# A two-layer conformer and attention trunk: a second half's products and sums of squares on VectorE, two early products ahead of the down projections

## The chip, the cores and the metric

The kernel runs on one core of a Trainium2 chip. Its time is device microseconds of one execution; given is the median of several executions. A core has five engines with an instruction stream each: TensorE (PE), VectorE (DVE), ScalarE (ACT), GpSimd (POOL) and SyncE (SP). Each issues its instructions in order and waits on semaphores for the others. Transfers are issued by SyncE (hardware queues) and by GpSimd (the software queue) and run beside the engines.

## The reference

A trunk of two layers over 512 tokens of width 1024, all in float32. Layer 0 is a conformer convolution and a SwiGLU feed-forward network (FFN); layer 1 is windowed attention over shared keys and values and a second FFN. The change touches the FFN of layer 0.

```python
def swiglu_ffn(x, w_up, w_down):
    gate, up = jnp.split(x @ w_up, 2, axis=-1)
    return (jax.nn.silu(gate) * up) @ w_down
...
def reference(...):
    h = x                                  # (1, 512, 1024) float32
    for l in range(2):
        if l < 1:
            h = h + conformer_conv(rmsnorm(h, norm_mix[l]), ...)   # pw1 + GLU, causal depthwise 31, LayerNorm, silu, pw2
        else:
            kv = rmsnorm(h, norm_kv) @ w_kv
            ...
            q = (rmsnorm(h, norm_mix[l]) @ w_q[j]).reshape(B, S, N_HEADS, HEAD_DIM)
            attn = banded_sink_attention(q, k_shared, v_shared, sinks[j], rel_bias)
            h = h + attn @ w_o[j]
        h = h + swiglu_ffn(rmsnorm(h, norm_ffn[l]), ffn_w_up[l], ffn_w_down[l])   # 1024 -> 2 x 2816 -> 1024
    return rmsnorm(h, norm_final)
```

## The kernel before

All activations stay on the chip, transposed (channels on the partitions, tokens along the free axis). Weights, about 250 MB of reads with their sums, are streamed in chunks of 128 x 1024 float32 (512 KB). A chunk goes through a fixed chain: SyncE loads it into one of six `raw` buffers (line 260; `load` runs nine chunks ahead of use), ScalarE casts it to the matmul's number format (`whi`, line 293), VectorE subtracts that from the original (`wlo`, line 296), at most three chunks ahead of use and with four buffers each, and TensorE multiplies. A product in full precision is three matmuls (`mm3`, lines 381 to 383): high weights by high activations, high weights by low activations, low weights by high activations. One chunk is 24 matmuls of 128x256. `PLAN` fixes the order of the chunks.

The FFN of layer 0 runs in this order. **Part 0**: the output projection of the convolution (`pw2`) and the ups, the gated product and the downs of hidden pairs 0 to 2, for the first 256 tokens. Then **twelve early products** (`FIRST`): pairs 3 to 10 are computed by a Strassen-like scheme of seven block products instead of eight (`SEVEN`); some of its products need the first half's tokens alone, and they are computed here and copied aside (line 1245). **Part 1**: `pw2` and pairs 0 to 2 for the second 256 tokens, in a "twin" form (`mm2`, two terms side by side). Then the remaining products of pairs 3 to 10 for all tokens, and their downs.

Behind TensorE run background jobs: a job is a generator, with points (chunk number, steps done) by which `pace` advances it. The convolution of the second half of tokens is such a job (`second`) during part 0 and the early products; `Rows0.sums`, which forms sums of activation blocks (`plain`, `rows`, lines 1283, 543, 546), is one during part 1.

The lines around the change:

- `evac` (lines 627 to 641) turns the banks of one pair into hidden activations. In the twin form: ScalarE copies half of a bank (632), VectorE adds the other (633), GpSimd multiplies by the inverse root mean square (635), ScalarE applies silu (636), GpSimd multiplies gate and up (637), ScalarE casts the high half (640), VectorE subtracts for the low half (641). Three pairs make six GpSimd products of 128x512.
- `Rms.add` (line 492) sums the squares of eight tiles for the norm, on the engine `eng` that it was given: GpSimd for the second half of tokens. Line 508 is the power that gives the inverse root mean square, on GpSimd.
- Four of the seven products use sums of weight blocks (`S1` to `S4`). They are formed in DRAM by transfers: a copy issued by SyncE (`copy_sums`, line 274) and a transfer that adds onto it, issued by GpSimd (`prepare`, line 288: `sum<-in_W` and `sum<-sum`). The latter is placed behind the last GpSimd operation that was marked by `pool_op`:

```python
            with tc.issue_after(pooled[0]):
                nc.gpsimd.dma_start(summed[c], chunk(c, SUMS[c[2]][1]), accum_op=ALU.add, max_dma_last_dim=4096)
```

Within these constraints a scheduler with a simulated timeline decides the order of the instructions of each engine.

Of the kernel before, what the change touches and what calls it, by code (L numbers as in the profile page):

```python
# [18 lines left out]
P = 128  # L19
# [18 lines left out]
FIRST = [(4, "A11"), (3, "A12"), (4, "A12"), (5, "A11"), (8, "A12"), (5, "A12"),  # L38
         (6, "A11"), (9, "A12"), (6, "A12"), (7, "A11"), (10, "A12"), (7, "A12")]
LAST = FT // 2 - 1  # L40
# [22 lines left out]
def ups(pair):  # L63
    return [("up", 0, pair, half, which) for half in range(2) for which in range(2)]
# [25 lines left out]
def chunk_plan():  # L90
# [7 lines left out]
    def downs(lo, hi):  # L98
        for g in range(2):
            for kp in range(lo, hi):  # L100
                plan.append(("down", 0, kp, g))

    for part in range(2):
        pw2()
        for pair in range(*HALVES0[0]):
            plan.extend(ups(pair))
        downs(*HALVES0[0])
        if part == 0:
            plan.extend(("up0", *step) for step in FIRST)
    for group in GROUPS0:  # L110
# [98 lines left out]
def hybrid_trunk(ctx: ExitStack, tc: tile.TileContext, xT, W, prm_in, wdw_in, sinks, relb, onehot, fin, lead, out):  # L209
# [54 lines left out]
    def pool_op(op):  # L264
        pooled[0] = op.ins
        return op
# [325 lines left out]

    def ffn_part(layer, part, xg, tok, rms, on_h=None, twin=False, plain=None):
        lo, hi = HALVES0[part]
        hid = ffn_up(layer, lo, hi, xg, tok, rms, twin, plain)
        w = tok.stop - tok.start
        for g in range(2):
# [22 lines left out]
    def ffn_up(layer, lo, hi, xg, tok, rms, twin=False, plain=None):  # L620
# [3 lines left out]
        def evac(pair, banks):  # L624
            rs_bc = rms.step2()
            if twin:
# [7 lines left out]
                t1v, t2v = (t.rearrange("p (a s) -> p a s", a=2) for t in (t1, t2))  # L634
                nc.gpsimd.tensor_mul(t1v, t1v, rs_bc.unsqueeze(1).to_broadcast([P, 2, w]))
                nc.scalar.activation(t1, t1, AF.Silu)
                pool_op(nc.gpsimd.tensor_mul(t2, t1, t2))
                i = 2 * (pair - lo)
# [268 lines left out]
    with tc.tile_pool(name="conv", bufs=2) as cv:  # L907
# [307 lines left out]
        with tc.issue_after(h0.silu):  # L1215
            late.gate()
        h1.after = [h0.silu]
        base = seen[0]
        job(second, (base, 0), (base + 8, 17), (base + 13, 20), (base + 26, 34), (base + 36, 40), (base + 39, 43), (base + 40, 44),
            (base + 41, 44), (base + 42, 45), (base + 43, 46), (base + 45, 48), (base + 46, 49), (base + 50, h1.n_steps - early))  # L1220
        x0 = {"ffn0": Pairs(KT)}
# [4 lines left out]
        preparing[0], share[0] = prepare(), 0.5  # L1226
        ffn_part(0, 0, x0["ffn0"], HALF[0], n0.rms, plain=plain)
        for _ in range(2):
            let_go()
        room = [q[:, n, :] for q in (quad(F32), quad(F32)) for n in range(4)]  # L1230
        room[4:4] = [keep.tile([P, 512], F32, tag="c11", name=uid("c11")) for _ in range(4)]
        room = [t.rearrange("p (a s) -> p a s", a=2) for t in room]
        first = {pair: {"A12": room[n]} for n, pair in enumerate(range(*HALVES0[1]))}
        for n, pair in enumerate(FIRST11):
            first[pair]["A11"] = room[8 + n]
        chains = {}
        for n, (pair, a) in enumerate(FIRST):
            pace()
            if n < 2:
                let_go()  # L1240
            begins = pair not in chains
            r = chains.setdefault(pair, new_chain() if begins else None)
            j = 4 * (a == "A12")
            product(("up0", pair, a), [[x0["ffn0"][j + k][e][:, HALF[0]] for k in range(4)] for e in range(2)], r, begins, pace)
            nc.scalar.copy(first[pair][a], r)  # L1245
        flush()
# [52 lines left out]
    plain1 = z0.tile([P, KT, W2], F32, tag="z0", name=uid("plain1"), bufs=4)  # L1299
    n1 = Next(("ffn0",), x0, bc0, HALF[1])  # L1300
    base = seen[0]
# [401 lines left out]
```

## Time and profile before

| | us |
|---|---|
| median of three runs | 1044.0 (1043.18, 1044.06, 1044.0) |
| profiled execution, its time | 1043.35 |
| profiled execution, its span | 1041.6 |
| TensorE busy | 1029.7 (99%) |
| VectorE busy | 794.5 (76%) |
| ScalarE busy | 603.4 (58%) |
| GpSimd busy | 455.3 (44%) |
| mean granted TensorE clock | 0.998 |

The span is what the profiler saw of that one execution; 1.75 us of its time lie outside it. A row of the timeline is start, duration, engine, line, operation, output<-input, and in brackets how long the engine had been idle and who released it. A busy TensorE counts matmuls whose ends are modelled and overlap, so what it lost is read from start to start. Part 0's downs begin at about 203 us, the early products follow them; the twin's ups end at about 303, and part 1's downs run on to about 330.

### The profile page before, as it was taken

To read this page: it belongs to the slowest core of one execution; us is meant where nothing else is said; L and a number is where in the kernel's file an instruction comes from. 1 tells how busy PE (TensorE), PEld (TensorE's weight loads), DVE (VectorE), ACT (ScalarE), POOL (GpSimd) and SP (SyncE) were. 2 spreads that over 40 slices of the span, in tenths; PEclk is the share of its full clock that TensorE was granted. 3 is DMA by queue.
4 is the path that set the end of the run, shared out by engine and by line. 5 is a ranking of instruction groups with operands and counts; after the bars stand their busy time and mean duration, and the time that the engine had idled before them with its cause. 6 is when DMAs were issued, how large, how long until landed. Compare 5 with 4: busy or idle time off the path is not lost.

```text
span 1041.6 us, 17905 instructions
## 1 busy us (share of the span) xinstructions
PE 1029.7 (99%) x6676; PEld 935.2 (90%) x6676; DVE 794.5 (76%) x1228; ACT 603.4 (58%) x1044; POOL 455.3 (44%) x557
## 2 busy tenths in 40 slices
PE   9999999999999999999999999999999999999996
PEld 8888889999989998899888877789989999898995
DVE  3999988986889795487567556678786877869686
ACT  3887796857574552256353555468645546554653
POOL 3999997752343233033234255501470333223134
PEclk9999999999999999999999999999999999999999
DMA  9999847999999999889998987977699897655642
GB/s 358 329 325 260 151 130 228 274 255 245 268 234 286 324 317 289 239 250 342 316 323 263 236 226 206 234 224 221 203 300 298 250 253 211 199 184 185 193 150 81
DMA packets 68243, 256.73 MB, mean 246 GB/s; under 512 B 7835, under 2 KB 14140, under 8 KB 67132
## 3 DMA queue, kind: packets, MB, share of 16 engines
q1 hardware_dynamic: 54044, 204.95, 57.0%
q0 software_dynamic: 13824, 50.34, 26.3%
q8 instruction: 52, 0.85, 0.3%
q10 hardware_dynamic: 288, 0.31, 0.1%
q14 instruction: 35, 0.29, 0.1%
HBM read 250.32 MB, written 105.91 MB: 342 GB/s over the span
## 4 chain that ended last, share of the span: by engine, by line
PE 94%; DVE 3%; DMA 2%; issue 1%; ACT 0%; POOLq 0%; POOL 0%; ACTq 0%; DVEq 0%
PE bank L381 20%; PE bank L382 20%; PE bank L383 20%; PE bank L933 10%; PE bank L878 9%; PE bank L379 4%; PE bank L413 2%; DMA raw<-sum 1%; PE bank L1437 1%; PE bank L1479 1%; PE bank L1466 1%; DVE wlo L296 1%; PE bank L414 1%; PE bank L1031 1%; PE bank L1612 1%
## 5 line engine op out<-in xcount | busy, mean ns | idle before, releaser
L293 ACT CAST whi<-raw 128x1024 fp32r<-128x1024 f32 x246 | 256.5, 1048 | 275.1 <-PE bank L382 181.0
L296 DVE TENSOR_TENSOR wlo<-raw,whi 128x1024 fp32r<-128x1024 f32 x246 | 317.6, 1299 | 117.3 <-ACT whi L293 116.5
L381 PE MATMUL bank<-quad,whi 128*128 128x256 f32 (+1 forms) x1016 | 315.8, 314 | 0.3 <-ACT quad L1245 0.2
L382 PE MATMUL bank<-quad,whi 128*128 128x256 f32 (+1 forms) x1016 | 315.5, 312 | 0.4 <-DVE quad L546 0.4
L383 PE MATMUL bank<-quad,wlo 128*128 128x256 f32 (+1 forms) x1016 | 314.5, 312 | 0.9 <-DVE wlo L296 0.9
L829 POOL TENSOR_TENSOR up<-up 128x512 f32<-128x512 f32 x38 | 71.8, 1889 | 345.9 <-ACT up L826 319.3
L381 PEld LDWEIGHTS bank<-quad,whi 128*128 128x128 f32 x1016 | 192.9, 191 | 13.1 <-issue 1.3
L383 PEld LDWEIGHTS bank<-quad,wlo 128*128 128x128 f32 x1016 | 193.0, 191 | 12.4 <-DVE wlo L296 1.1
L382 PEld LDWEIGHTS bank<-quad,whi 128*128 128x128 f32 x1016 | 193.4, 191 | 11.6 <-DVE quad L546 0.6
L975 POOL TENSOR_TENSOR pr<-pr,pr 128x256 f32<-128x256 f32 x208 | 155.4, 794 | 6.6 <-ACT pr L974 6.5
L381 PE MATMUL bank<-rows,whi 128*128 128x256 f32 x544 | 154.0, 284 | 0.7 <-ACT whi L293 0.4
L382 PE MATMUL bank<-rows,whi 128*128 128x256 f32 x544 | 153.6, 283 | 0.0
L383 PE MATMUL bank<-rows,wlo 128*128 128x256 f32 x544 | 153.4, 283 | 0.0
L982 DVE SCALAR_TENSOR_TENSOR bank<-apad,wdw,bank 128x256 f32<-128x256 f32 x248 | 112.4, 485 | 3.3
L974 ACT ACTIVATE pr<-apad,wdw 128x256 f32<-128x256 f32 x208 | 98.2, 501 | 14.6 <-POOL pr L975 12.7
L381 PEld LDWEIGHTS bank<-rows,whi 128*128 128x128 f32 x544 | 103.5, 191 | 1.9 <-ACT whi L293 0.6
L382 PEld LDWEIGHTS bank<-rows,whi 128*128 128x128 f32 x544 | 103.7, 191 | 0.5 <-issue 0.2
L383 PEld LDWEIGHTS bank<-rows,wlo 128*128 128x128 f32 x544 | 103.6, 191 | 0.0
L933 PE MATMUL bank<-quad,w 128*128 128x256 f32 x448 | 98.7, 380 | 0.0
L933 PEld LDWEIGHTS bank<-quad,w 128*128 128x128 f32 x448 | 84.9, 190 | 11.8 <-DVE bank L982 0.2
L878 PE MATMUL bank<-wlo,fhi 128*128 128x512 f32 x140 | 55.3, 395 | 0.0
L492 POOL TENSOR_TENSOR tmp<-tmp,tmp 128x256 f32<-128x256 f32 (+1 forms) x28 | 27.1, 969 | 64.3 <-ACT tmp L488 58.6
(231 smaller groups left out, 1550.3 us busy)
## 6 DMA issues: line engine op xcount, KB each, us to landing
raw<-in_W_dram SPq DMA_DIRECT2D x162, 512.0 KB, 5.8
raw<-sum SPq DMA_DIRECT2D x96, 512.0 KB, 4.7
sum<-in_W_dram SPq DMA_DIRECT2D x64, 512.0 KB, 7.6
sum<-in_W_dram POOLq DMA_DIRECT2D x48, 512.0 KB, 8.9
sum<-sum POOLq DMA_DIRECT2D x48, 512.0 KB, 10.3
sum<-in_W_dram SPq DMA_DIRECT2D x4, 4096.0 KB, 34.6
w<-in_W_dram SPq DMA_DIRECT2D x14, 512.0 KB, 8.9
fd<-fs SPq DMA_DIRECT2D x1, 3072.0 KB, 44.7
```

Source lines behind the costliest of these rows:

```text
L293: on_act = nc.scalar.copy(hi, src).ins
L296: latest[:] = [on_act, lo_engine[0].tensor_sub(lo, src, f32(hi)).ins]
L379: stamp[0] = nc.tensor.matmul(out, w[0], x, start=start, stop=stop).ins
L381: nc.tensor.matmul(out, w[0], x[0], start=start, stop=False, **kw)
L382: nc.tensor.matmul(out, w[0], x[1], start=False, stop=False, **kw)
L383: stamp[0] = nc.tensor.matmul(out, w[1], x[0], start=False, stop=stop, **kw).ins
L829: pool_op(nc.gpsimd.tensor_mul(gate, gate, c[:, m, :, 1, :]))
L878: nc.tensor.matmul(out, x, w[:, ws], start=first and e == 0 and i == 0, stop=e == 1 and i == 2, skip_group_check=True)
L933: mm = nc.tensor.matmul(self.pb[:, w * W2:(w + 1) * W2], w1_of(ct, w, k), x[k] if x else xg[k][:, tok], start=k == 0, stop=k == KT - 1)
L974: on_act = nc.scalar.mul(pr, a[:, j:j + W2], tap(j))
L975: on_pool = pool_op(nc.gpsimd.tensor_add(pr, acc, pr))
L982: on_dve = nc.vector.scalar_tensor_tensor(yt if i == nd - 1 else c, src, tap(i), c if i else self.shift, op0=ALU.mult, op1=ALU.add)
```

## The change

Four edits. The twin's two GpSimd products in `evac` become VectorE products, and the second of them is no longer marked by `pool_op`. The sums of squares of the second half (`n1`) are added by VectorE, and with that they too are not marked. Two of the early products run between the ups and the downs of part 0 (`mid`), the other ten behind the downs, one of them, (7, A11), two places earlier. The points of the second half's convolution between 20 and 36 steps are given in more detail. Line numbers behind the edits shift by 3 to 13.

```diff
--- before.py
+++ after.py
@@ -36,7 +36,8 @@
 GROUPS0 = ((3, 7), (7, 11))
 FIRST11 = (4, 5, 6, 7)
 FIRST = [(4, "A11"), (3, "A12"), (4, "A12"), (5, "A11"), (8, "A12"), (5, "A12"),
-         (6, "A11"), (9, "A12"), (6, "A12"), (7, "A11"), (10, "A12"), (7, "A12")]
+         (6, "A11"), (7, "A11"), (9, "A12"), (6, "A12"), (10, "A12"), (7, "A12")]
+N_MID = 2
 LAST = FT // 2 - 1
 STEPS1 = [("two", 0), ("up", 2), ("low", 0)]
 TWO = [(p, a) for a in ("A11", "A12", "S4") for p in range(2)] + [(p, a) for p in range(2) for a in ("S1", "S2", "S3", "A22")]
@@ -104,9 +105,11 @@
         pw2()
         for pair in range(*HALVES0[0]):
             plan.extend(ups(pair))
+        if part == 0:
+            plan.extend(("up0", *step) for step in FIRST[:N_MID])
         downs(*HALVES0[0])
         if part == 0:
-            plan.extend(("up0", *step) for step in FIRST)
+            plan.extend(("up0", *step) for step in FIRST[N_MID:])
     for group in GROUPS0:
         plan.extend(("up0", *step) for step in part2_products(group))
         downs(*group)
@@ -590,9 +593,11 @@
         nc.vector.tensor_mul(b, b, rs_bc)
         nc.vector.tensor_add(into, b, into)
 
-    def ffn_part(layer, part, xg, tok, rms, on_h=None, twin=False, plain=None):
+    def ffn_part(layer, part, xg, tok, rms, on_h=None, twin=False, plain=None, mid=None):
         lo, hi = HALVES0[part]
         hid = ffn_up(layer, lo, hi, xg, tok, rms, twin, plain)
+        if mid is not None:
+            mid()
         w = tok.stop - tok.start
         for g in range(2):
             if w == 256:
@@ -632,9 +637,9 @@
                         nc.scalar.copy(tm, b[:, 1, :])
                         nc.vector.tensor_add(tm, b[:, 0, :], tm)
                 t1v, t2v = (t.rearrange("p (a s) -> p a s", a=2) for t in (t1, t2))
-                nc.gpsimd.tensor_mul(t1v, t1v, rs_bc.unsqueeze(1).to_broadcast([P, 2, w]))
+                nc.vector.tensor_mul(t1v, t1v, rs_bc.unsqueeze(1).to_broadcast([P, 2, w]))
                 nc.scalar.activation(t1, t1, AF.Silu)
-                pool_op(nc.gpsimd.tensor_mul(t2, t1, t2))
+                nc.vector.tensor_mul(t2, t1, t2)
                 i = 2 * (pair - lo)
                 q = hid.q[i // 4][:, i % 4:i % 4 + 2]
                 nc.scalar.copy(q[:, :, 0, :], t2v)
@@ -1216,33 +1221,41 @@
             late.gate()
         h1.after = [h0.silu]
         base = seen[0]
-        job(second, (base, 0), (base + 8, 17), (base + 13, 20), (base + 26, 34), (base + 36, 40), (base + 39, 43), (base + 40, 44),
-            (base + 41, 44), (base + 42, 45), (base + 43, 46), (base + 45, 48), (base + 46, 49), (base + 50, h1.n_steps - early))
+        job(second, (base, 0), (base + 8, 17), (base + 13, 20), (base + 20, 27), (base + 24, 30), (base + 30, 36), (base + 36, 40),
+            (base + 39, 43), (base + 40, 44), (base + 41, 44), (base + 42, 45), (base + 43, 46), (base + 45, 48), (base + 46, 49),
+            (base + 50, h1.n_steps - early))
         x0 = {"ffn0": Pairs(KT)}
         plain = quads.tile([P, KT, W2], F32, tag="quad", name=uid("plain"))
         bc0 = new_bc()
         n0 = Next(("ffn0",), x0, bc0, HALF[0], nc.vector, plain)
         pw2(h0.z, n0)
         preparing[0], share[0] = prepare(), 0.5
-        ffn_part(0, 0, x0["ffn0"], HALF[0], n0.rms, plain=plain)
+        first, chains = {}, {}
+
+        def early_products(steps):
+            for pair, a in steps:
+                pace()
+                if held:
+                    let_go()
+                begins = pair not in chains
+                r = chains.setdefault(pair, new_chain() if begins else None)
+                k0 = 4 * (a == "A12")
+                product(("up0", pair, a), [[x0["ffn0"][k0 + k][e][:, HALF[0]] for k in range(4)] for e in range(2)], r, begins, pace)
+                nc.scalar.copy(first[pair][a], r)
+
+        def mid():
+            room = [q[:, n, :] for q in (quad(F32), quad(F32)) for n in range(4)]
+            room[4:4] = [keep.tile([P, 512], F32, tag="c11", name=uid("c11")) for _ in range(4)]
+            room = [t.rearrange("p (a s) -> p a s", a=2) for t in room]
+            first.update((pair, {"A12": room[n]}) for n, pair in enumerate(range(*HALVES0[1])))
+            for n, pair in enumerate(FIRST11):
+                first[pair]["A11"] = room[8 + n]
+            early_products(FIRST[:N_MID])
+
+        ffn_part(0, 0, x0["ffn0"], HALF[0], n0.rms, plain=plain, mid=mid)
         for _ in range(2):
             let_go()
-        room = [q[:, n, :] for q in (quad(F32), quad(F32)) for n in range(4)]
-        room[4:4] = [keep.tile([P, 512], F32, tag="c11", name=uid("c11")) for _ in range(4)]
-        room = [t.rearrange("p (a s) -> p a s", a=2) for t in room]
-        first = {pair: {"A12": room[n]} for n, pair in enumerate(range(*HALVES0[1]))}
-        for n, pair in enumerate(FIRST11):
-            first[pair]["A11"] = room[8 + n]
-        chains = {}
-        for n, (pair, a) in enumerate(FIRST):
-            pace()
-            if n < 2:
-                let_go()
-            begins = pair not in chains
-            r = chains.setdefault(pair, new_chain() if begins else None)
-            j = 4 * (a == "A12")
-            product(("up0", pair, a), [[x0["ffn0"][j + k][e][:, HALF[0]] for k in range(4)] for e in range(2)], r, begins, pace)
-            nc.scalar.copy(first[pair][a], r)
+        early_products(FIRST[N_MID:])
         flush()
 
     bias = {}
@@ -1297,7 +1310,7 @@
     part2 = ExitStack()
     z0 = part2.enter_context(tc.tile_pool(name="part2", bufs=4))
     plain1 = z0.tile([P, KT, W2], F32, tag="z0", name=uid("plain1"), bufs=4)
-    n1 = Next(("ffn0",), x0, bc0, HALF[1])
+    n1 = Next(("ffn0",), x0, bc0, HALF[1], nc.vector)
     base = seen[0]
     rows0 = Rows0(x0["ffn0"], plain, plain1)
     rows0.rms = rows0
```

The order of the instructions shows what this moves. A number behind a name counts tiles: whi_3586 and wlo_3587 are the high and the low part of one chunk. The chunks around the end of part 1 are called by running numbers: 46 to 48 (the last of them whi_3521) and 49 to 51 (whi_3553, whi_3586, whi_3625) are part 1's downs, for the first and for the second half of the output channels; 52 (whi_3656) and 53 (whi_3687) are the first chunks of the products that follow.

GpSimd, from the power of the second half's norm (rs_3214) through the twin. Before:

```order
L288 DMA sum_512<-sum_508 128x1024
L508 TENSOR_TENSOR rs_3214<-ms_3212,mhalf 128x2
L288 DMA sum_506<-in_W_dram 128x1024
L635 TENSOR_TENSOR tmp_3271<-tmp_3271,rsbc_1401 128x512
L637 TENSOR_TENSOR tmp_3272<-tmp_3271,tmp_3272 128x512
L288 DMA sum_510<-in_W_dram 128x1024
L288 DMA sum_508<-sum_506 128x1024
L635 TENSOR_TENSOR tmp_3389<-tmp_3389,rsbc_1401 128x512
L637 TENSOR_TENSOR tmp_3390<-tmp_3389,tmp_3390 128x512
L288 DMA sum_512<-sum_508 128x1024
L288 DMA sum_506<-in_W_dram 128x1024
L635 TENSOR_TENSOR tmp_3502<-tmp_3502,rsbc_1401 128x512
```

Now:

```order
L291 DMA sum_512<-sum_508 128x1024
L511 TENSOR_TENSOR rs_3214<-ms_3212,mhalf 128x2
L291 DMA sum_506<-in_W_dram 128x1024
L291 DMA sum_510<-in_W_dram 128x1024
L291 DMA sum_508<-sum_506 128x1024
L291 DMA sum_512<-sum_508 128x1024
L291 DMA sum_506<-in_W_dram 128x1024
L291 DMA sum_510<-in_W_dram 128x1024
L291 DMA sum_779<-in_W_dram 128x1024
L291 DMA sum_510<-in_W_dram 128x1024
L291 DMA sum_508<-sum_506 128x1024
L291 DMA sum_512<-sum_508 128x1024
```

The products between the transfers are gone; from rs_3214 to the first gate of the next stage eleven accumulating transfers follow one another, and nine, with no computation between them, stand ahead of it.

VectorE, in part 1's downs (wlo_3554 is chunk 49's low half, quad_3159 the last pair's hidden activations). Before:

```order
L296 TENSOR_TENSOR wlo_3522<-raw_3339,whi_3521 128x1024
L1283 TENSOR_TENSOR plain_2862<-plain_2862 128x1024
L633 TENSOR_TENSOR tmp_3503<-bank_3406,tmp_3503 128x256
L633 TENSOR_TENSOR tmp_3503<-bank_3407,tmp_3503 128x256
L296 TENSOR_TENSOR wlo_3554<-raw_3364,whi_3553 128x1024
L546 TENSOR_TENSOR rows_3557<-plain_2862,rows_3557 128x1024
L296 TENSOR_TENSOR wlo_3587<-raw_3408,whi_3586 128x1024
L641 TENSOR_TENSOR quad_3159<-tmp_3503,quad_3159 128x2x256
```

Now:

```order
L299 TENSOR_TENSOR wlo_3522<-raw_3339,whi_3521 128x1024
L1296 TENSOR_TENSOR plain_2862<-plain_2862 128x1024
L638 TENSOR_TENSOR tmp_3503<-bank_3406,tmp_3503 128x256
L638 TENSOR_TENSOR tmp_3503<-bank_3407,tmp_3503 128x256
L640 TENSOR_TENSOR tmp_3502<-tmp_3502,rsbc_1401 128x512
L299 TENSOR_TENSOR wlo_3554<-raw_3364,whi_3553 128x1024
L299 TENSOR_TENSOR wlo_3587<-raw_3408,whi_3586 128x1024
L549 TENSOR_TENSOR rows_3557<-plain_2862,rows_3557 128x1024
L642 TENSOR_TENSOR tmp_3503<-tmp_3502,tmp_3503 128x512
L299 TENSOR_TENSOR wlo_3626<-raw_3431,whi_3625 128x1024
```

The products of line 640 and 642 stand among the subtractions, and the two subtractions of chunks 49 and 50 follow one another.

TensorE, in part 1's downs, from the end of chunk 50 (whi_3586) on. Before:

```order
L383 MATMUL bank_3619<-quad_3158,wlo_3587 128x256
L381 MATMUL bank_3619<-quad_3158,whi_3586 128x256
L382 MATMUL bank_3619<-quad_3158,whi_3586 128x256
L383 MATMUL bank_3619<-quad_3158,wlo_3587 128x256
L381 MATMUL bank_3618<-quad_3159,whi_3625 128x256
L382 MATMUL bank_3618<-quad_3159,whi_3625 128x256
```

Now:

```order
L385 MATMUL bank_3619<-quad_3158,whi_3586 128x256
L386 MATMUL bank_3619<-quad_3158,wlo_3587 128x256
L384 MATMUL bank_3724<-quad_1396,whi_3656 128x256
L385 MATMUL bank_3724<-quad_1396,whi_3656 128x256
L384 MATMUL bank_3517<-quad_3159,whi_3521 128x256
L384 MATMUL bank_3518<-quad_3159,whi_3521 128x256
L384 MATMUL bank_3618<-quad_3159,whi_3625 128x256
L384 MATMUL bank_3619<-quad_3159,whi_3625 128x256
L384 MATMUL bank_3756<-rows_3370,whi_3687 128x256
L385 MATMUL bank_3756<-rows_3370,whi_3687 128x256
L386 MATMUL bank_3724<-quad_1396,wlo_3657 128x256
```

Before, chunk 51 (whi_3625) and chunk 52 followed in full, and chunk 53 (whi_3687) behind both; now two matmuls each of 52, 48 (whi_3521), 51 and 53 come first.

## The prediction

> **What bounds the kernel now.** I read the page first: its busy times, and the shares of the chain of waits.
>
> ```profile
> PE 1029.7 (99%) x6676; PEld 935.2 (90%) x6676; DVE 794.5 (76%) x1228; ACT 603.4 (58%) x1044; POOL 455.3 (44%) x557
> PE 94%; DVE 3%; DMA 2%; issue 1%; ACT 0%; POOLq 0%; POOL 0%; ACTq 0%; DVEq 0%
> ```
>
> TensorE bounds it. The change adds and removes no matmul, so it can only move the time in which TensorE stands still. The second view is the list of TensorE's waits, the third the windows by stage, of the one stage that is undisturbed and of the ones the change touches.
>
> ```profile
> PE bank L383 <- DVE wlo L296: 0.9, 1, 0.9
> PE bank L382 <- DVE quad L546: 0.4, 1, 0.4
> PE bank L381 <- ACT whi L293: 0.4, 1, 0.4
> PE bank L381 <- ACT quad L1245: 0.2, 1, 0.2
> 200.00:205.00 5.00, 4.63 (x38) 4.30 (x37) 5.00 (x8) 4.90 (x10) 4.44 (x6) 1.00 0.95 223
> 215.00:220.00 5.00, 5.00 (x44) 5.00 (x43) 5.00 (x7) 2.68 (x5) 4.52 (x5) 1.00 1.02 344
> 315.00:320.00 5.00, 4.07 (x34) 3.81 (x32) 5.00 (x5) 3.04 (x4) 3.11 (x3) 1.00 1.02 334
> 335.00:340.00 5.00, 4.51 (x35) 3.93 (x33) 2.50 (x4) 1.54 (x2) 0.00 (x0) 1.00 1.06 271
> ```
>
> The columns are length, then busy time and count for TensorE, weight loads, VectorE, ScalarE and GpSimd, granted clock, DMA share, GB/s. A full window holds 44 matmuls at clock 1.00, one each 0.114 to 0.12 us; a weight chunk of 24 matmuls therefore takes 2.88 us. In 315:320 VectorE is busy all 5.00 us and TensorE misses ten matmuls. The timeline of TensorE has the holes one by one:
>
> ```profile
> 202.78 0.28 PE L382 MATMUL bank<-quad,whi 128*128 128x256 f32 x1
> 203.43 0.38 PE L382 MATMUL bank<-quad,whi 128*128 128x256 f32 x1 [0.37 <-DVE quad L546]
> 230.78 0.28 PE L383 MATMUL bank<-quad,wlo 128*128 128x256 f32 x1
> 231.23 0.39 PE L381 MATMUL bank<-quad,whi 128*128 128x256 f32 x1 [0.17 <-ACT quad L1245]
> 317.25 0.28 PE L382 MATMUL bank<-quad,whi 128*128 128x256 f32 x1
> 318.46 0.39 PE L383 MATMUL bank<-quad,wlo 128*128 128x256 f32 x1 [0.93 <-DVE wlo L296]
> 338.73 0.28 PE L383 MATMUL bank<-rows,wlo 128*128 128x256 f32 x1
> 339.43 0.39 PE L381 MATMUL bank<-rows,whi 128*128 128x256 f32 x1 [0.42 <-ACT whi L293]
> ```
>
> Start to start minus the usual 0.12, they lose 0.53, 0.33, 1.09 and 0.58 us. The matmul behind a hole starts its successor 0.22 us later instead of 0.12, which adds 0.1 each: 0.6, 0.4, 1.2 and 0.7. A few smaller gaps lie beside the last three in these windows; from the missing matmuls I count 0.1, 0, 0.3 and 0.5 for them. So what the change can win here is 0.7 + 0.4 + 1.5 + 1.2 = 3.8 us of 1041.6, about 0.4%.
>
> **First part: two early products ahead of the downs.** The hole at 203 waits for the low half of the last pair's hidden activations. Between that pair's ups and the downs now run two products, 2 x 2.88 = 5.8 us of matmuls on data that was complete before. They cover a hole of 0.6. The same two are missing later, between the downs and the second part, where nothing was waited for that they hid: the rest of the list keeps ten. The hole at 231 is the copy of an early product standing late in ScalarE's order; with the new list that copy is issued ahead of the squares. I count both as gone, -0.7 and -0.4. If the cover fails they stay (0), and that is one bound; a product that itself waits for its weights would be the other, at most the 0.58 of the weight wait seen at 339 for each, +1.2. Weights are the reason against: at 200 to 230 loads land in 5.8 us, with nine chunks (25.9 us) issued ahead. The earlier job points of the second half's convolution move ScalarE and VectorE work by a few chunks inside 220 to 265; the full window there (x44 in 215:220) says that TensorE does not notice, so 0, with the 0.4 of the hole at 231 as its bound.
>
> ```profile
> raw<-in_W_dram SPq DMA_DIRECT2D x11, 512.0 KB, 5.8
> ```
>
> **Second part: six products and seven adds go from GpSimd to VectorE.** The price of one comes from the same shapes on VectorE, the relief from VectorE rows that overlap a GpSimd product:
>
> ```profile
> L641 DVE TENSOR_TENSOR quad<-tmp,quad 128x512 fp32r<-128x512 f32 x3 | 2.0, 679 | 0.0
> 294.38 1.47 DVE L296 TENSOR_TENSOR wlo<-raw,whi 128x1024 fp32r<-128x1024 f32 x1 [0.80 <-ACT whi L293]
> 298.16 1.66 DVE L1283 TENSOR_TENSOR t<-plain,plain 128x1024 f32<-128x1024 f32 x1
> 299.75 3.05 DVE L296 TENSOR_TENSOR wlo<-raw,whi 128x1024 fp32r<-128x1024 f32 x1
> 305.34 2.14 POOL L637 TENSOR_TENSOR tmp<-tmp,tmp 128x512 f32<-128x512 f32 x1 [3.64 <-DVE tmp L633]
> 306.25 2.31 DVE L1283 TENSOR_TENSOR plain<-plain,t 128x1024 f32<-128x1024 f32 x1
> 313.32 2.21 POOL L635 TENSOR_TENSOR tmp<-tmp,rsbc 128x512 f32<-128x512 f32 x1 [4.22 <-DVE tmp L633]
> 314.29 2.32 DVE L1283 TENSOR_TENSOR plain<-plain 128x1024 f32<-128x1024 f32 x1
> 317.42 2.13 POOL L637 TENSOR_TENSOR tmp<-tmp,tmp 128x512 f32<-128x512 f32 x1 [1.89 <-DVE tmp L633]
> 318.32 2.31 DVE L546 TENSOR_TENSOR rows<-plain,rows 128x1024 fp32r<-128x1024 f32 x1
> 323.43 1.21 DVE L1283 TENSOR_TENSOR plain<-plain 128x1024 f32<-128x1024 f32 x1
> ```
>
> A 128x512 operation is 0.68 us, 0.60 from start to start in a run of them: six cost VectorE 3.6 us. In exchange, a 1.21 us operation lasted 2.31 whenever it met a GpSimd product, and ended about 1.1 us behind it. Three of them give back 3.3 us; the lengthened operations at 294.38, 298.16 and 299.75 give 0.26, 0.45 and 1.84 more, against 1.21. Net: 3.6 - 5.8 = -2.2 us on VectorE in 290 to 325. Bounds: +3.6 without any relief, -2.2 with all of it. I take the whole relief, since each lengthened row lies beside a product; most of it falls early, where the subtractions are chunks ahead. The products also get shorter in their own chain (0.68 for some 2.1 of GpSimd), though each now stands in VectorE's order behind a weight's subtraction of 1.21, so the hidden pair is not later.
>
> The low weights that TensorE waits for at 317.25 are subtracted in VectorE's next-but-one place. There the operation at 314.29 shrinks by 1.1 and one product, 0.6, slips in ahead of that subtraction: in sum it ends some 0.8 us earlier than the 318.4 of before, still 0.2 to 0.3 late. TensorE also arrives earlier by what it won before, 1.1, which VectorE follows only in part. So of the 1.5 lost around 318 I take back 1.5 and put a remainder of 0.3 against it: bounds 0 and 1.5.
>
> The seven adds of squares (128x256) cost half of a product's 0.68 each, 2.4 us in all, around 268 to 283; the GpSimd adds there lengthened VectorE's neighbours:
>
> ```profile
> L538 DVE SCALAR_TENSOR_TENSOR quad<-h,prm,quad 128x256 fp32r<-128x256 f32 x8 | 6.8, 899 | 0.0
> L982 DVE SCALAR_TENSOR_TENSOR bank<-apad,wdw,bank 128x256 f32<-128x256 f32 x19 | 9.1, 479 | 0.1
> ```
>
> Against 479 ns the eight of L538 hold 8 x 0.42 = 3.4 us, of which I count 2 as contention. Nothing of TensorE waits here, so 0; without the relief +2.4 of VectorE time in front of chunks that are several ahead, still 0 for TensorE unless the lead is gone (below).
>
> **The accumulating transfers.** GpSimd issues the sums of weight blocks (`sum<-in_W`, `sum<-sum`) in its own order. Six of them stood behind the last product at 317.42 and left in one burst:
>
> ```profile
> 319.50 0.82 POOL L288 DMA_DIRECT2D sum<-in_W_dram  x1
> 322.15 2.38 POOL L288 DMA_DIRECT2D sum<-sum  x1
> 338.32 1.05 ACT L293 CAST whi<-raw 128x1024 fp32r<-128x1024 f32 x1 [4.35 <-DMA raw<-sum]
> 342.13 1.05 ACT L293 CAST whi<-raw 128x1024 fp32r<-128x1024 f32 x1 [2.26 <-DMA raw<-in_W_dram]
> 345.94 1.05 ACT L293 CAST whi<-raw 128x1024 fp32r<-128x1024 f32 x1 [2.27 <-DMA raw<-sum]
> raw<-sum SPq DMA_DIRECT2D x7, 512.0 KB, 15.2
> ```
>
> While they run, a weight chunk arrives every 3.81 us (338.32, 342.13, 345.94) for 2.88 of use, and its load takes 15.2 us (the last row, transfers issued in 320 to 345). In the changed order GpSimd computes nothing between 240 and 345 except one 128x2 power: nine transfers stand ahead of it, eleven behind, held only by what they read. They start earlier and are through some 15 us sooner, around 333, so that the weights for 338 land in time: -1.2. Bounds: 0, and the starvation of rival C.
>
> **A new wait.** TensorE's order at the end of part 1 changes: behind chunk 50 (whi 3586) come only six matmuls of other chunks and then chunk 53 (whi 3687), which stood 72 matmuls later. There are four buffers of high weights, and the cast of 53 needs the one of 50. Its load is the first of the four here:
>
> ```profile
> 311.46 10.66 SPq L260 DMA_DIRECT2D raw<-sum  x4
> DMA to landing us min/median/max: 6.8/10.3/17.3
> ```
>
> (the second row is all loads of raw weights issued in 308 to 332). TensorE reaches the place 45 matmuls after 317.25, at 322.65, less 1.1 won before, plus 0.3: 321.85. Landing is 311.46 + 10.3 = 321.8. The cast, 1.05 with 0.1 on each side, ends at 323.1, while six matmuls last until 322.6: 0.5 is the lower bound. At 17.3 us to land it would be 7.3. With more accumulating transfers in flight at that point than before, I take 1.1, near the median.
>
> **The sum.** -0.7 - 0.4 - 1.5 - 1.2 + 0.3 + 1.1 = -2.4 us. The profiled execution took 1043.35 us (span 1041.6), 0.65 under the median 1044.0 of three (1043.18 to 1044.06). So 1040.95 for such an execution and **1041.6 us** for the median.
>
> **The rivals.** A is the forecast. **B: the gain is eaten at chunk 53.** If its load takes 12.5 us rather than 10.3 to 11, TensorE waits 2.7 there and not 1.1: net -0.8, 1043.2. For it: the same view's maximum of 17.3 and the DMA share near 1.0 throughout; against it: the four loads of that row left one after the other as buffers came free, so an earlier VectorE also issues them earlier.
>
> **C: twenty accumulates in one stream starve the weights, slower.** At 3.81 us per chunk from 287 to 329, 11.0 chunks arrive and 14.6 are used: 3.6 chunks or 10.3 us of matmuls must come out of the lead. The lead is 25.9 us of issue-ahead less 15.2 to land, 10.7, if all nine may be in flight; six raw buffers alone, 17.3, leave 2.1. With a lead of 4, a wait of 6.3 arises: 6.3 - 2.4 = +3.9, 1047.9. It decides against the change from a lead under 7.9, and measurably under 5.8. For it: 15.2 against 5.8 us to land. Against it: a transfer that adds to a sum waits for the one before it, so the eleven cannot all run at once, and in 315:320 with four of them queued the only wait was VectorE's. The Trainium skill's page "DMA: Bandwidth & Descriptors", section "Queues, rings and completion order", says that each DMA engine serves the queues it has work for in turn, a packet at a time. By that the software queue takes its share from the weights as long as it has anything to do, whoever is urgent; the trace agrees so far, in the landing times just named.
>
> **D: VectorE becomes the bound, slower.** If the lengthened operations stay long for another reason, VectorE does 3.6 us more before the low weights at 318: the 1.5 there becomes 5.1 instead of 0.3, net -2.4 + 4.8 = +2.4, 1046.4. For it: 5.00 of 5.00 busy in 315:320. Against it: 1.21 us at 323.43 once no product ran.
>
> That the change does not do what it says is no case: the orders show both moves.
>
> **How the numbers follow.** Two readings closer than 0.2%, 2.1 us, cannot be told apart for this kernel, so faster is under 1041.9 and slower over 1046.1. A 0.60 (0.52 faster, 0.08 same, as 1041.6 stands close to the line), B 0.19 (0.16 same, 0.03 faster if the wait is only a little larger), C 0.13 and D 0.08 (0.20 slower between them, 0.01 same). Faster 0.55, same 0.25, slower 0.20. The low end is no new wait beyond 0.5 and a remainder of 0: 1041.6 - 0.6 - 0.3, and 1.0 more of the smaller gaps in these windows, 1039.7. The high end takes in B and D's 1046.4: 1046.5, with C beyond it. The forecast's own range is 1039.7 to 1042.8.
>
> **What would show it.** Right: no TensorE wait for the hidden low half near the first downs, none for an early product's copy, 128x1024 operations of VectorE at 1.21 all through the twin, accumulating transfers gone from 319 to 323, no ScalarE wait of over 2 us for a weight at 338, and a short TensorE wait for a cast of high weights at about 322. Wrong: a wait of more than 2 us for `raw<-sum` between 315 and 335 (B or C), TensorE waiting for `wlo` with VectorE at 5.00 of 5 (D), or holes in the same places as before.

## The result and the profile after

The change made the kernel slower: 1048.16 us median of six runs (1047.41 to 1048.84) against 1043.63 for the kernel before on the same chip (1043.18 to 1044.06), a ratio of 1.0043 (95% interval 1.003 to 1.0056), +4.5 us. The forecast was 1041.6 with a range up to 1046.5. The profiled execution, the slowest of the six, took 1048.84 us; its span is 1047.0.

The page's busy times and chain, then the list of TensorE's waits (who waits, for whom; sum, times, longest):

```profile
PE 1032.8 (99%) x6676; PEld 938.1 (90%) x6676; DVE 793.7 (76%) x1241; ACT 603.9 (58%) x1044; POOL 436.9 (42%) x544
PE 96%; DMA 2%; DVE 1%; issue 0%; ACT 0%; POOLq 0%; SPq 0%; POOL 0%; DVEq 0%; ACTq 0%
```

```profile
PE bank L384 <- ACT whi L296: 2.5, 1, 2.5
PE bank L533 <- ACT tmp L519: 1.7, 1, 1.7
```

The waits for low weights (0.9), for the hidden pair's low half (0.4) and for the early product's copy (0.2) are no longer in this list. Two others have come, 2.5 and 1.7 us. The windows say where, and what came behind them; first two of the kernel before, then the change:

```profile
290.00:295.00 5.00, 5.00 (x30) 4.39 (x29) 3.33 (x6) 4.35 (x10) 1.28 (x1) 1.00 1.07 292
330.00:335.00 5.00, 5.00 (x45) 5.00 (x44) 5.00 (x7) 2.10 (x2) 0.00 (x0) 1.00 1.03 300
```

```profile
200.00:205.00 5.00, 5.00 (x44) 5.00 (x43) 5.00 (x9) 4.18 (x7) 5.00 (x6) 1.00 0.86 277
285.00:290.00 5.00, 3.78 (x24) 3.10 (x22) 2.47 (x4) 2.23 (x3) 1.23 (x2) 1.00 0.83 265
290.00:295.00 5.00, 4.49 (x17) 3.85 (x18) 2.54 (x5) 4.98 (x15) 5.00 (x7) 0.66 0.90 172
315.00:320.00 5.00, 5.00 (x43) 5.00 (x42) 5.00 (x7) 3.39 (x5) 0.00 (x0) 1.00 1.08 277
325.00:330.00 5.00, 2.46 (x20) 2.21 (x19) 1.84 (x3) 2.66 (x4) 0.00 (x0) 1.00 1.07 278
330.00:335.00 5.00, 4.99 (x29) 4.99 (x30) 2.85 (x4) 1.64 (x3) 0.00 (x0) 0.66 1.03 373
335.00:340.00 5.00, 5.00 (x44) 5.00 (x44) 4.79 (x7) 1.64 (x3) 0.00 (x0) 1.00 0.98 398
```

The three stages with holes, 200, 315 and 335, are full (43 and 44 matmuls). Both new waits are followed by a window at a granted clock of 0.66, with 17 and 29 matmuls where the kernel before has 30 and 45. In this execution each wait costs a second time, in the slower matmuls behind it; the experiments show that the first of the two need not.

The first wait, by the rows of each engine in turn:

```profile
287.35 0.50 PE L507 MATMUL bank<-ones_c,tmp 128*128 128x1 f32 x4
288.38 0.40 PE L417 MATMUL bank<-quad,whi 128*128 128x512 f32 x1
290.51 1.22 PE L533 MATMUL bank<-tmp,ones_m 128*128 128x256 f32 x2 [1.73 <-ACT tmp L519]
288.53 0.15 DVE L509 TENSOR_SCALAR ms<-bank 128x2 f32<-128x2 f32 x1
288.77 0.71 POOL L511 TENSOR_TENSOR rs<-ms,mhalf 128x2 f32<-128x2 f32 x1 [25.77 <-DVE ms L509]
288.82 1.04 ACT L296 CAST whi<-raw 128x1024 fp32r<-128x1024 f32 x1 [1.46 <-PE bank L417]
289.77 0.69 ACT L519 ACTIVATE tmp<-ident,rs 128x128 f32<-128x128 f32 x2
```

TensorE sums the squares (L507), and some 1.2 us later it wants to spread the norm over the partitions (L533). Between them lie VectorE, the power on GpSimd, and the diagonal on ScalarE (L519), which stands behind a cast that itself waited for a buffer of TensorE's. Start to start 2.13 us pass.

The second wait is for chunk 53 (its first matmul is the last row on TensorE). Behind it, the two casts before that matmul, the load of chunk 53 as a link of the chain (start, length), and the transfers that GpSimd had issued:

```profile
326.72 0.74 PE L384 MATMUL bank<-quad,whi 128*128 128x256 f32 x4
330.01 0.39 PE L384 MATMUL bank<-rows,whi 128*128 128x256 f32 x1 [2.55 <-ACT whi L296]
325.10 1.05 ACT L296 CAST whi<-raw 128x1024 fp32r<-128x1024 f32 x1 [2.57 <-DMA raw<-in_W_dram]
328.91 1.04 ACT L296 CAST whi<-raw 128x1024 fp32r<-128x1024 f32 x1 [2.25 <-DMA raw<-sum]
313.69 15.14 DMA raw<-sum
289.45 1.71 POOL L291 DMA_DIRECT2D sum<-in_W_dram  x2
290.56 2.31 POOL L291 DMA_DIRECT2D sum<-sum  x2
291.60 3.78 POOL L291 DMA_DIRECT2D sum<-in_W_dram  x3
```

Seven accumulating transfers left within 3.2 us of the power, and weights came 3.81 us apart (325.10, 328.91). The transfers issued in 300 to 325, first of the kernel before and then of the change (share of 16 engines' time for the software queue; loads, their size, median us to landing):

```profile
q0 software_dynamic: 676, 2.49, 60.8%
raw<-sum SPq DMA_DIRECT2D x5, 512.0 KB, 9.2
```

```profile
q0 software_dynamic: 1023, 3.73, 74.9%
raw<-sum SPq DMA_DIRECT2D x5, 512.0 KB, 16.0
```

To add this up I took, for each profiled execution, the distance from the start of each matmul to that of the next, less the usual one for its form, by stage:

| us lost by TensorE | 195-235 | 286-315 | 315-345 |
|---|---|---|---|
| before | 2.20 | 0.29 | 2.80 |
| the change | 1.15 | 3.81 | 4.40 |

The stage 286 to 315 holds the twin's ups; their last matmul starts at 310.9 in the kernel before, not at about 303.

Of the holes 3.85 us are gone (1.05 in the first stage, all of the 2.80 in the last); the two new waits with their slow matmuls cost 3.5 and 4.4 us. The rest of the 5.4 us between the spans lies mostly in the kernel's start (0.5) and in 170 to 195 (0.7), where five kernels below that leave this stage as it was (`r_only`, `t_only`, `t_no_hoist`, `t_paced`, `r_paced`) lose anything from 1.68 to 2.89.

### The profile page after: what moved, and what is told of

It reads as the page before. It is cut to its first block, busy times and chain, and to the rows that moved or that the text cites. A ratio compares the mean times of both kernels' runs of the same rounds, so it can differ in the third digit from the quotient of the medians.

```text
span 1047.0 us, 17895 instructions
## 1 busy us (share of the span) xinstructions
PE 1032.8 (99%) x6676; PEld 938.1 (90%) x6676; DVE 793.7 (76%) x1241; ACT 603.9 (58%) x1044; POOL 436.9 (42%) x544
## 4 chain that ended last, share of the span: by engine, by line
PE 96%; DMA 2%; DVE 1%; issue 0%; ACT 0%; POOLq 0%; SPq 0%; POOL 0%; DVEq 0%; ACTq 0%
PE bank L384 21%; PE bank L386 21%; PE bank L385 21%; PE bank L938 10%; PE bank L883 9%; PE bank L382 4%; PE bank L416 2%; DMA raw<-sum 1%; PE bank L1450 1%; PE bank L1492 1%; PE bank L1479 1%; PE bank L417 1%; PE bank L1036 1%; PE bank L1625 1%; DMA both<-in_lead_dram 1%; PE bank L926 1%
## 5 line engine op out<-in xcount | busy, mean ns | idle before, releaser
L291 POOL DMA_DIRECT2D sum<-sum x48 | 47.7, 1103 | 34.3 <-DMA sum<-sum 18.8
```

## The experiments

R stands for the seven adds on VectorE, T for the six products, M for the early products, their order and the job points. Theory A puts both waits down to TensorE's new order alone, theory Q to the stream of accumulating transfers. Medians are us, the kernel before beside them from the same chip.

**First set: each part alone, and the order of chunk 53 undone.** The edits are the lines of the change one at a time. `t_no_hoist` adds to T:

```diff
-            open_pairs[pair].take(a)
+            with tc.issue_after(stamp[0]) if (pair, a) in part2_products(GROUPS0[0])[:2] else nullcontext():
+                open_pairs[pair].take(a)
```

> Only the seven adds of squares of the second half move to VectorE; all else as before. Theory A (order): TensorE's matmul that sums the squares (L504) now stands 6 rows ahead of the spread of the norm (L530) instead of 16, so TensorE waits for the power, the turned diagonal and the casts between, about 1.9 us and then some 1.3 us at a lowered clock, near 288: 3.2 to 3.5 us slower than before, nothing new at 325, the old holes at 203, 231 and 318 unchanged: 1046.5 to 1047.5. Rival Q (transfers): the loss comes from the accumulating transfers that lost their markers and bunch at 241 to 262, so late weights show as several waits for high weights between 262 and 300, of any place. Rival N (neutral): within 0.5 us of before.

> Only the six products of the twin move to VectorE. Theory A: the order of TensorE puts chunk 53 six matmuls behind chunk 50, and TensorE waits there for its load, 2.5 to 4.4 us with the lowered clock after it, against 1.5 won at 318 and 1.2 at 339: 0 to 1.7 us slower, 1043.6 to 1045.3; no wait at 288. Rival D (VectorE bound): a wait for low weights at 318 of over 1 us stays. Rival N: all of the gain, 1041.

> Only the two early products between ups and downs, the list's new order and the job points; products and sums of squares on GpSimd as before. Theory A: the holes at 203 and 231 go, 0.7 + 0.4 - 0.1, the hole at 318 stays: 1042.6, 1.0 us faster than before. Rival: the middle products or the moved background cost what they save, 1043.6.

> As t_only, with the first two products of the next stage held behind the downs in TensorE's order, so that chunk 53 is used 72 matmuls later. Theory A: no wait of over 0.5 us between 315 and 340, 1.5 + 1.2 - 0.3 won: 1041.2, faster than t_only by 2 to 4 us. Rival Q (the twenty transfers in one stream starve the weights whatever the order): waits for high weights of 2 us or more move on to chunks behind 53, and the time stays within 1 us of t_only.

| kernel | median | before | ratio (95%) | 195-235 | 286-315 | 315-345 |
|---|---|---|---|---|---|---|
| r_only | 1044.72 | 1043.49 | 1.0009 (1.0 to 1.0019) | 1.80 | 2.38 | 1.13 |
| t_only | 1046.67 | 1043.49 | 1.0038 (1.0024 to 1.0051) | 1.77 | 0.37 | 4.71 |
| m_only | 1042.64 | 1043.49 | 0.9993 (0.9985 to 1.0002) | 0.87 | 0.37 | 1.86 |
| t_no_hoist | 1046.28 | 1043.49 | 1.0026 (1.0017 to 1.0036) | 2.07 | 0.29 | 5.98 |

The longest waits in the lists of `r_only` and of `t_only`, and the window behind the wait of `r_only`:

```profile
PE bank L530 <- ACT tmp L516: 1.7, 1, 1.7
PE bank L381 <- ACT whi L293: 2.5, 1, 2.5
290.00:295.00 5.00, 3.88 (x21) 3.41 (x22) 2.64 (x5) 5.00 (x15) 0.93 (x2) 1.00 0.90 236
```

Each new wait belongs to one part: the one at 288 to R, the one at chunk 53 to T. R alone costs less than I expected, for two reasons. The clock behind its wait stayed at 1.00, so the stage lost 2.38 and not 3.81; and the holes of 315 to 345 shrank by 1.7 while TensorE stood still earlier. T alone came out 1.4 us above the upper end that I had given; its last stage lost 1.9 more than before, and the rest lies mostly in stages that its edit does not touch. M removes the holes of 195 to 235; its profiled execution lost 1.8 us more in 170 to 195, and its ratio does not exclude 1.

The fourth kernel threw theory A over for chunk 53. Chunk 53 was wanted 72 matmuls later, and the time hardly moved. In its list of waits:

```profile
PE bank L381 <- ACT quad L640: 2.9, 1, 2.9
```

And in ScalarE's timeline:

```profile
316.75 1.05 ACT L293 CAST whi<-raw 128x1024 fp32r<-128x1024 f32 x1 [2.77 <-DMA raw<-in_W_dram]
320.57 1.05 ACT L293 CAST whi<-raw 128x1024 fp32r<-128x1024 f32 x1 [1.28 <-DMA raw<-in_W_dram]
324.35 1.04 ACT L293 CAST whi<-raw 128x1024 fp32r<-128x1024 f32 x1 [2.21 <-DMA raw<-in_W_dram]
325.30 0.61 ACT L640 CAST quad<-tmp 128x512 fp32r<-128x512 f32 x1
328.15 1.05 ACT L293 CAST whi<-raw 128x1024 fp32r<-128x1024 f32 x1 [2.24 <-DMA raw<-sum]
```

Four casts, 3.8 us apart, each waiting for its load. The cast of the last pair's activations (325.30) stood behind one of them in ScalarE's order, and TensorE waited 2.9 us for that. So the weights are late, and the order decides only which matmul finds it out.

**Second set: the stream itself.** `t_paced` leaves T and its order alone and gives the transfers something to stand behind on GpSimd:

```diff
                 nc.vector.tensor_mul(t2, t1, t2)
+                pool_op(nc.gpsimd.tensor_copy(small.tile([P, 1], F32, tag="mark", name=uid("mark")), t2[:, 0:1]))
```

`r_late_spread` is R with the twin's first eviction cut in two, its second part (from the norm's spread on) run a chunk later:

```diff
...
-                t1v, t2v = (t.rearrange("p (a s) -> p a s", a=2) for t in (t1, t2))
+                def finish():
+                    rs_bc = rms.step2()
+                    t1v, t2v = (t.rearrange("p (a s) -> p a s", a=2) for t in (t1, t2))
...
+                late.append(finish)
+                if pair > lo:
+                    late.pop()()
...
+                    if late and half == 0 and which == 0:
+                        late.pop()()
```

`after_even` is the whole change with a copy of the newest low weights ahead of each accumulating transfer of part 1, and `after_even_late` has the late spread as well:

```diff
+            if paced[0]:
+                pool_op(nc.gpsimd.tensor_copy(small.tile([P, 1], F32, tag="mark", name=uid("mark")), f32(lows[-1][:, 0:1])))
             with tc.issue_after(pooled[0]):
                 nc.gpsimd.dma_start(summed[c], ...
```

> As t_only with TensorE's order unchanged (chunk 53 six matmuls behind chunk 50); added: GpSimd copies one 128x1 column of each pair's gated product, so that the accumulating transfers behind it in its order leave when they left before, not in one stream. Theory Q (the stream starves the weights): casts of high weights no longer arrive every 3.8 us at 316 to 328, TensorE's wait for chunk 53 falls from 2.5 us to under 1.2: 1042.5 to 1043.5, 3 us faster than t_only. Theory A (order alone): the wait stays at 2 us or more, 1046.

> As r_only, with the spread of the norm moved one chunk of the twin later in TensorE's order (28 rows later); the accumulating transfers as in r_only. Theory A for this wait (distance from the sums of squares to the spread in TensorE's order): no TensorE wait at 288, 1.9 to 2.3 us less lost there than in r_only: 1042.5. Theory Q for this wait (late weights make the squares late whatever the order): TensorE waits as long at the new place or at another within 285 to 300, 1044.5.

> The whole change, but from the second half's projection to the end of the twin each accumulating transfer waits for a GpSimd copy of one column of the low weights that were split last, so one leaves per two chunks. Theory Q: no weight casts 3.8 us apart at 300 to 330, the wait for chunk 53 under 1 us; the wait for the spread at 288 stays, 1.9 to 3.5 us: 1043.0 to 1044.5, 4 to 5 us faster than the change. Theory A: both waits stay, 1048.

> As after_even, and with the spread of the norm one chunk later. If both causes are named rightly: no TensorE wait of over 0.6 us between 195 and 345: 1040.5 to 1041.5, faster than both kernels by 2 us or more. If one is not: 1043 or more.

| kernel | median | before | ratio (95%) | 195-235 | 286-315 | 315-345 |
|---|---|---|---|---|---|---|
| t_paced | 1041.43 | 1043.53 | 0.998 (0.9971 to 0.9988) | 1.91 | 0.29 | 0.56 |
| r_late_spread | 1046.8 | 1043.53 | 1.0033 (1.0021 to 1.0045) | 1.95 | 0.37 | 5.80 |
| after_even | 1045.97 | 1043.53 | 1.0023 (1.0013 to 1.0034) | 1.65 | 5.89 | 0.00 |
| after_even_late | 1042.6 | 1043.53 | 0.9993 (0.9984 to 1.0001) | 1.67 | 2.80 | 0.10 |

`t_paced` is T with the same order on TensorE, VectorE and ScalarE and the same six products on VectorE; only the copies, and with them the times at which transfers leave, differ. It is 5.2 us under `t_only`, faster than the kernel before, and 1.1 below the range that I had given. Its wait for chunk 53, and its software queue and loads in 300 to 325:

```profile
PE bank L381 <- ACT whi L293: 0.3, 1, 0.3
```

```profile
q0 software_dynamic: 584, 2.13, 51.1%
raw<-sum SPq DMA_DIRECT2D x5, 512.0 KB, 8.5
```

Theory Q holds for chunk 53. For the spread it does not: in `r_late_spread`, with the transfers up to there as in `r_only`, the wait at 288 is gone (0.37), so that one is the order. The time did not follow. TensorE, no longer held up at 288, came to the weights behind the burst of six transfers that this kernel still has at 320 before they were there. Its waits, the first at 339; the second is the old one for low weights, since its products are still on GpSimd:

```profile
PE bank L381 <- ACT whi L293: 2.2, 1, 2.2
PE bank L383 <- DVE wlo L296: 1.1, 1, 1.1
```

The cast that the first one was for began at 340.78. In the kernel before, with the same burst, it began at 338.32 and TensorE waited 0.4. Why it came 2.5 us later here is not shown; the late spread also moved the twin's products on GpSimd, and with them four transfers (two left at 299 and two at 307 to 308 in the kernel before, all four at 304 to 307 here).

Pacing by chunks took away all that was lost in 315 to 345, but one of the copies and the transfer behind it now stand ahead of the power of the norm in GpSimd's order, and the power itself took 1.96 us (from 288.57 on) instead of the 0.71 of the change. So in `after_even` the wait at 288 grew to 3.7 us, which I had not expected. With the late spread it is gone, and the low halves of the first two pairs' hidden activations come late instead, of which 2.0 us are waited for at 311 and 315:

```profile
PE bank L389 <- DVE quad L653: 2.0, 2, 1.4
```

**Third set: the causes taken out of the change one at a time.** `after_paced` is the whole change with the copy of `t_paced`; `tm` is the change without R; `tm_paced` without R and with the copy; `r_paced` is R with a copy behind each add:

```diff
                 if self.eng is nc.gpsimd:
                     pool_op(op)
+                elif len(preparing) > 1:
+                    pool_op(nc.gpsimd.tensor_copy(small.tile([P, 1], F32, tag="mark", name=uid("mark")), sq[:, 0:1]))
...
+    preparing.append(None)
```

The last line, placed behind the second half's `n1`, is the flag that the `elif` asks for.

> The whole change, with the accumulating transfers of the twin paced as in t_paced (GpSimd copies one column of each gated product ahead of them); TensorE's order as in the change. Theory Q: the wait for chunk 53 near 326 falls from 2.6 us (4.4 lost with the lowered clock) to under 0.7, the wait for the spread near 288 (3.5 lost) stays: 1044 to 1045, 3 to 4 us faster than the change. Theory A (order alone): both stay, 1048.

> The whole change without the seven adds of squares, which go back to GpSimd. TensorE's order at 288 is the old one. Theory: no wait at 288 (3.5 less lost), the wait for chunk 53 stays with its lowered clock: 1045 to 1046.5. Rival: the wait at 288 comes from the moved early products, 1048.

> The whole change without the seven adds, and with the twin's accumulating transfers paced. If both losses are named rightly, nothing of them is left and the holes at 203, 231, 318 and 339 are gone: 1040 to 1041, faster than before by 2.5 to 3.5 us and than t_paced by some 0.8. If the early products cost elsewhere what they save (m_only lost 1.8 us near 181 in its profiled execution): 1041.5 to 1042.5.

> As r_only, with a GpSimd copy of one column behind each of the seven adds, so that the accumulating transfers of 241 to 286 leave as before; TensorE's order as in r_only (6 rows from the sums of squares to the spread). Order theory for the wait at 288: it stays at 1 us or more, 1044 to 1045. Stream theory (late weights make the squares late): it falls below 0.5 us, 1042.5.

| kernel | median | before | ratio (95%) | 195-235 | 286-315 | 315-345 |
|---|---|---|---|---|---|---|
| after_paced | 1044.2 | 1043.45 | 1.0004 (0.9995 to 1.0013) | 0.91 | 2.38 | 0.56 |
| tm | 1047.1 | 1043.45 | 1.0035 (1.0021 to 1.0049) | 0.97 | 0.37 | 5.94 |
| tm_paced | 1040.88 | 1043.45 | 0.9977 (0.9968 to 0.9986) | 1.28 | 0.29 | 0.56 |
| r_paced | 1044.21 | 1043.45 | 1.0007 (0.9998 to 1.0016) | 1.73 | 2.38 | 0.59 |

In `r_paced` the transfers left later again and ScalarE's casts were in time. The last cast ahead of the squares, in `r_only` and then in `r_paced`:

```profile
279.90 1.05 ACT L293 CAST whi<-raw 128x1024 fp32r<-128x1024 f32 x1 [3.91 <-DMA raw<-in_W_dram]
278.49 1.05 ACT L293 CAST whi<-raw 128x1024 fp32r<-128x1024 f32 x1 [1.79 <-PE bank L382]
```

The wait for the spread is the same 1.7 us to the tenth (its timeline of TensorE):

```profile
288.87 0.50 PE L506 MATMUL bank<-ones_c,tmp 128*128 128x1 f32 x4
292.03 0.70 PE L532 MATMUL bank<-tmp,ones_m 128*128 128x256 f32 x2 [1.73 <-ACT tmp L518]
```

So the wait at 288 is R's order, and the late weights that also showed there in the change's trace did not set it. For `tm` I had expected 1045 to 1046.5; it came out at 1047.1, with a further wait of 1.2 us for chunk 52's cast (1.4 from start to start). `tm_paced` is full at each of the places:

```profile
285.00:290.00 5.00, 5.00 (x32) 4.42 (x31) 1.48 (x3) 3.69 (x10) 1.54 (x2) 1.00 1.05 306
315.00:320.00 5.00, 5.00 (x44) 5.00 (x43) 5.00 (x6) 3.38 (x6) 1.26 (x2) 1.00 1.04 253
330.00:335.00 5.00, 5.00 (x44) 5.00 (x44) 5.00 (x8) 1.82 (x3) 0.00 (x0) 1.00 1.04 272
```

It beats both kernels: 2.6 us under the one before, and by the two ratios some 0.66% under the change. What M adds to T with the copy is not settled: 0.9977 against 0.998 for `t_paced`, with intervals that overlap.

## Why the prediction was wrong

**First part, the holes at 203 and 231.** Right. 1.05 us of the forecast 1.1 were won; `m_only` won 1.33 there.

**VectorE in the twin.** Right. The lengthened operations are short again and the wait for low weights is gone; I had left 0.3 of it. From VectorE's timeline of the change, the two that had lasted 2.32 and 2.31:

```profile
315.98 1.22 DVE L1296 TENSOR_TENSOR plain<-plain 128x1024 f32<-128x1024 f32 x1
320.65 1.22 DVE L549 TENSOR_TENSOR rows<-plain,rows 128x1024 fp32r<-128x1024 f32 x1
```

Rival D falls with that.

**The step that failed first: "Nothing of TensorE waits here, so 0" for the seven adds.** I costed them as VectorE time, and that was indeed harmless. But they moved the matmul that sums the squares ten rows later in TensorE's order and left the spread where it was: the spread is now the sixth row behind it where it was the sixteenth. The chain through VectorE, GpSimd and ScalarE needs about 3.2 us from the sums (287.35 to 290.51), and the sums with the five rows behind them cover little over 1. The missing term was 1.9 us of wait. With what lies beside it the stage lost 2.1 more than before in `r_only`, `after_paced` and `r_paced`, and 3.5 in the change's profiled execution, where slow matmuls came behind it. The order itself showed the distance, and I did not lay the chain's length against it.

**The step that was mis-sized: the wait at chunk 53, 1.1.** The place was right, and what came last there was the load. I timed it with 10.3 us, the median of before, though I had written that the transfers would leave earlier and in one stream; this load took 15.1, and the median of its kind was 16.0. It also left at 313.69 and not at 311.46, so it landed at 328.8 and not at 321.8. TensorE, held up at 288, came 4.7 us later than I had timed it, which hid the larger part of that delay. Rival B's wait of 2.7 is what TensorE lost from start to start, and rival C's mechanism is what caused it. Its 1047.9 is near the measured 1048.16, though by other shares: it had one wait of 6.3, and there were two. I gave it 0.13, on the argument that a transfer which adds to a sum waits for the one before it. Seven of them left within 3.2 us all the same: each adds onto a sum of its own, and they took 8.6 to 27.5 us to land.

**What no term held: the lowered clock.** All windows of 5 us of the kernel before that I had read (170 to 350) granted 1.00, and I priced each wait at its own length. In the change's profiled execution the two new ones cost 3.5 and 4.4 us for 1.9 and 2.7 of waiting. At 288 that is not the price of the order alone: the last section has three kernels with the same wait and the full clock.

**The accumulating transfers, -1.2 at 339.** The hole did go, but as `t_paced` shows it goes even with the six transfers still leaving at 320 to 324: there the raw buffers came free earlier because VectorE subtracted earlier. The load behind that hole left at 320.46, not at 323.53, each just behind the end of a subtraction. My reason, that the burst disappears, was not needed.

## What to carry to other kernels

Moving work off an engine also moves what is queued behind it. Where transfers are placed behind computation on a queue, that computation paces them, and a copy of one column can keep the pace when the work leaves, as long as nothing urgent stands behind the copy. Where an edit shifts one end of a chain across several engines, lay the chain's length against the distance that is left in the order of the engine that waits for it, whatever the moved work itself costs.

## What the hardware showed

With accumulating transfers of the software queue in flight, a 512 KB load of weights came every 3.8 us in each kernel that let them bunch, and without them four loads in a row landed 1.25 us apart (268 to 273 in the kernel before, behind the last transfer of its first burst at 267.7). So about one accumulating transfer passes for each load. By the Trainium skill's page "DMA: Bandwidth & Descriptors", section "Queues, rings and completion order", the DMA engines serve their queues in turn; the trace agrees with 3.8 us per pair, and pacing the software queue is what helped.

The granted clock fell to 0.66 for the window behind the change's two waits of 2.13 and 2.83 us from start to start. The Trainium skill's page "TensorE: Matmul & The Clock Gate", section "Part 1: The HAM clock gate (the "warmup" mystery)", gives an idle window of about 3.4 us for that. Here shorter waits were enough, though not always. Behind the waits that the lists give as 2.2 us or more (in `t_only`, `t_no_hoist`, `tm`, `r_late_spread` and `after_even`) the clock fell too, to between 0.51 and 0.82 in the first window of 5 us that shows it. But `r_only`, `after_paced` and `r_paced` waited the same 2.13 us as the change at the same place and kept 1.00 there. What decides between the two no run here shows.
